# A decoder trunk on one core: softmax on negated scores, the sink as a column, one broadcast scaling, rotary's second product in one operation

## The chip, the core and the metric

The kernel runs on one core of a Trainium2 chip. The core's engines work side by side, each on a queue of its own in a fixed order: PE multiplies matrices, DVE does elementwise work and reductions, ACT evaluates functions and copies, POOL does elementwise work too, and SP issues the loads. They meet only where one waits for another's result. The metric is the device time of one execution in microseconds, the median of the runs.

## The reference, cut to what matters

Two layers over 256 tokens of width 1024, float32. Each is a half SwiGLU, a token mixer, a half SwiGLU, all on RMS-normed input with residuals. Layer 0 mixes with native sparse attention (16 heads of 64 in four groups; a compressed, a selected and a sliding-window branch with keys and values of their own, each weighted by a sigmoid gate). Layer 1 mixes with sliding-window attention of window 128, two key heads, and a sink logit per head:

```python
x1, x2 = jnp.split(x, 2, axis=-1)                       # rotary
out = jnp.concatenate([x1 * c - x2 * s, x2 * c + x1 * s], axis=-1)
...
s = jnp.where(mask, einsum(q, k) * scale, NEG)          # softmax with a sink
m = jnp.maximum(jnp.max(s, axis=-1, keepdims=True), sk)
e = jnp.exp(s - m)
p = e / (jnp.sum(e, axis=-1, keepdims=True) + jnp.exp(sk - m))
```

With 256 tokens, all of the selected blocks are taken, so the selected branch is causal attention over all keys, and so is the window of 512.

## The kernel before

The residual stays on chip, tokens on the partitions, in two tiles of 128 rows (`t` = 0, 1). Every large product runs on PE as three products of operands split into a high and a low part. A weight piece of 128x1024 is loaded by SP, its high part is cast (L150, mostly ACT), and its low part is a subtraction (L175), on DVE in one instruction or on POOL in two of 128x512. The names tell the product: `gu` and `dn` are the two of a SwiGLU, `nin`, `cmp`, `nout` the input, compression and output products of the first attention, `sin`, `sout` those of the second.

An attention layer is a list of steps in the code. `R` is a chunk of the input projection; `P` and `V` (or `A`) turn its result into rotated, transposed queries and keys by `rope` (L382) and `token_split`; `S` is `logits` (L425) for a group of four heads and a tile of rows; `M` is `weigh` and `heads_sum`, the products with the values. In the first layer `S` works on two branches (`nb` = 2, tiles `na_p`), in the second on one (`sa_p`). There are eight `S` steps in either layer, four groups by two tiles; a row is 128 keys long for `t` = 0 and 256 for `t` = 1.

Within `logits`: PE writes scores to PSUM (`na_s`, `sa_s`); for each head and branch one DVE instruction adds the mask, writes to SBUF and takes the row's greatest value (L443); a bias step makes the negated, scaled greatest value (L633 in the first layer; L741, L742, L744 with the sink in the second, and L745 for the sink's exponential on ACT); ACT takes one exponential a head, with its sum (L451); a scale step makes the reciprocal of the sums (and in the first layer multiplies by the gates, L636 and L638; in the second L749 adds the sink's exponential ahead of L750's reciprocal); then one scaling a head and branch (L461, or L459 on ACT) in place, mostly on DVE, some on POOL or ACT by a table. PE then transposes the probabilities (`na_t`, `sa_t`), ACT and DVE split them (`na_h`, `na_l`), PE multiplies with the values (`na_o`, `sa_o`).

A scheduler sets the order of every engine's queue when the kernel is built, from the order in the code, numbers on the steps that let them yield, and what depends on what. Between the `S` steps it places other work on the same queues: the weights' subtractions, the compression's GELU (`hid`, `ge_a`, `ge_b`, and `hidT`, the transpose on PE that follows it), the probabilities of the compressed branch (`cm`), rotary for the next group. At the start of each layer POOL raises the mean square to the power -1/2 (`n_y`, L231), and DVE makes the row scale and rotary's tables from it.

## Time and profile before

| | |
|---|---|
| median of 3 runs | 1046.49 us (1043.96 to 1047.28) |
| span of the profiled execution, first to last instruction | 1040.8 us; the profile gives no other time for it |
| PE busy | 997.2 us, 96% |
| DVE, ACT, POOL busy | 719.4, 554.7, 518.0 us |
| mean granted PE clock | 0.981 |
| first attention layer, about | 201 to 382 us |
| second attention layer, about | 751 to 848 us |

A row of the instruction views gives the start, the duration, the engine and line, the operation, the tiles written and read, and how many were merged; in brackets stands the engine's idle time before it and who ended it. Durations of neighbours on DVE overlap a little, so the distance between starts is what an instruction costs its queue. A row of the stretches gives the length, each engine's busy time in the order PE, weight loads, DVE, ACT, POOL, then the PE clock as a share of full speed and the DMA's share and rate.

### The profile page before, as it was taken

How to read it: one execution, taken by the hardware profiler on the slowest of the kernel's cores; microseconds unless marked ns; L12 is line 12 of the kernel's file. 1: busy time of each engine (PE TensorE's matmuls, PEld its weight loads, DVE VectorE, ACT ScalarE, POOL GpSimd, SP SyncE). 2: the span in 40 equal slices, each digit the busy share in tenths (PEclk: the TensorE clock that was granted, in tenths of full speed). 3: DMA queues.
4: the chain of work that ended last, by engine and by line, in shares of the span. 5: the costliest groups of instructions: out<-in, count | busy, mean ns of one | idle time of the engine just before them, and what ended most of it. 6: DMA issues, size and time to landing. Idle time of an engine off the chain costs nothing.

```text
span 1040.8 us, 16105 instructions
## 1 busy us (share of the span) xinstructions
PE 997.2 (96%) x5663; PEld 860.2 (83%) x5663; DVE 719.4 (69%) x1418; ACT 554.7 (53%) x1049; POOL 518.0 (50%) x504
## 2 busy tenths in 40 slices
PE   6999999998789999999999999999998899999996
PEld 5888888898778678888888888888897688888896
DVE  6777744478788987777445777754289888777533
ACT  5555544356458755565444555544457755555432
POOL 1675563457253417655631555572665326554543
PEclk9999999999889999999999999999999999999999
DMA  8665655533220336655555556546542156555551
GB/s 275 194 200 187 197 185 176 176 123 122 82 82 1 122 131 194 202 185 186 184 185 191 181 187 199 187 159 222 176 149 61 61 184 199 183 184 186 187 174 41
DMA packets 47328, 169.10 MB, mean 162 GB/s; under 512 B 5264, under 2 KB 5776, under 8 KB 47248
## 3 DMA queue, kind: packets, MB, share of 16 engines
q1 hardware_dynamic: 46512, 166.37, 49.8%
q10 hardware_dynamic: 576, 1.20, 0.4%
q8 instruction: 44, 0.72, 0.3%
q0 software_dynamic: 160, 0.52, 0.1%
q14 instruction: 36, 0.29, 0.1%
HBM read 167.02 MB, written 1.05 MB: 161 GB/s over the span
## 4 chain that ended last, share of the span: by engine, by line
PE 85%; DVE 8%; ACT 2%; POOL 2%; issue 2%; DMA 1%; POOLq 0%; DVEq 0%; ACTq 0%
PE gu L116 47%; PE dn L116 22%; PE nin L116 5%; DVE na_p L461 2%; PE nout L116 2%; PE na_o L116 2%; PE sout L116 1%; PE xt L191 1%; DVE sa_p L461 1%; PE sin L116 1%; PE na_s L116 1%; PE na_t L470 1%; ACT sa_p L451 1%; DMA x<-in_x_dram 1%; DVE sa_p L443 1%
## 5 line engine op out<-in xcount | busy, mean ns | idle before, releaser
L116 PE MATMUL gu<-xh,gu_h 128*128 128x512 f32 x1408 | 492.4, 396 | 2.8 <-DVE xh L200 2.8
L116 PE MATMUL gu<-xh,gu_l 128*128 128x256 f32 x1408 | 393.8, 280 | 0.0
L116 PEld LDWEIGHTS gu<-xh,gu_h 128*128 128x128 f32 x1408 | 264.8, 188 | 63.6 <-DVE xh L200 3.2
L116 PEld LDWEIGHTS gu<-xh,gu_l 128*128 128x128 f32 x1408 | 266.2, 189 | 0.5
L175 DVE TENSOR_TENSOR gu_l<-gu_r,gu_h 128x1024 fp32r<-128x1024 f32 (+1 forms) x177 | 237.4, 1342 | 27.0 <-ACT gu_h L150 26.7
L150 ACT CAST gu_h<-gu_r 128x1024 fp32r<-128x1024 f32 (+1 forms) x177 | 184.7, 1044 | 44.5 <-PE gu L116 21.8
L150 ACT CAST dn_h<-dn_r 128x1024 fp32r<-128x1024 f32 (+1 forms) x89 | 92.2, 1041 | 110.1 <-PE dn L116 102.6
L116 PE MATMUL dn<-dn_l,hh 128*128 128x512 f32 (+1 forms) x396 | 147.0, 371 | 0.0
L116 PE MATMUL dn<-dn_h,hh 128*128 128x512 f32 (+1 forms) x396 | 146.9, 371 | 0.0
L116 PE MATMUL dn<-dn_h,hl 128*128 128x512 f32 (+1 forms) x396 | 146.6, 370 | 0.0
L175 DVE TENSOR_TENSOR dn_l<-dn_r,dn_h 128x1024 fp32r<-128x1024 f32 (+1 forms) x56 | 72.1, 1291 | 99.6 <-ACT dn_h L150 99.6
L175 POOL TENSOR_TENSOR dn_l<-dn_r,dn_h 128x512 fp32r<-128x512 f32 x66 | 88.8, 1367 | 104.3 <-ACT dn_h L150 94.5
L155 POOL TENSOR_TENSOR ga<-g,rb 128x256 f32<-128x256 f32 x88 | 96.8, 1100 | 71.0 <-DVE g L356 48.5
L155 POOL TENSOR_TENSOR hl<-u,hh 128x256 fp32r<-128x256 f32 x66 | 80.3, 1217 | 49.9 <-ACT hh L150 25.3
L155 POOL TENSOR_TENSOR u<-u,rb 128x256 f32<-128x256 f32 x88 | 70.1, 796 | 66.6 <-DVE u L358 66.6
L360 ACT ACTIVATE th<-ga 128x256 f32<-128x256 f32 x88 | 36.8, 419 | 99.1 <-POOL ga L155 98.1
L116 PEld LDWEIGHTS dn<-dn_h,hl 128*128 128x128 f32 x396 | 74.8, 189 | 13.4
L116 PEld LDWEIGHTS dn<-dn_h,hh 128*128 128x128 f32 x396 | 74.7, 189 | 13.4
L116 PEld LDWEIGHTS dn<-dn_l,hh 128*128 128x128 f32 x396 | 74.8, 189 | 13.2
L150 ACT COPY g<-gu 128x256 f32<-128x256 f32 x88 | 32.7, 372 | 83.4 <-PE gu L116 82.8
L116 PE MATMUL nin<-nin_h,xh 128*128 128x256 f32 (+1 forms) x352 | 72.9, 302 | 1.4 <-DVE r_b L389 1.4
L362 DVE SCALAR_TENSOR_TENSOR ga<-th,ga 128x256 f32<-128x256 f32 x88 | 43.2, 491 | 36.2 <-ACT th L360 36.2
(243 smaller groups left out, 1483.5 us busy)
## 6 DMA issues: line engine op xcount, KB each, us to landing
gu_r<-in_wgu_dram SPq DMA_DIRECT2D x175, 512.0 KB, 4.1
dn_r<-in_wdn_dram SPq DMA_DIRECT2D x87, 512.0 KB, 3.5
nin_r<-in_nsa_in_dram SPq DMA_DIRECT2D x20, 512.0 KB, 3.5
sin_r<-in_swa_in_dram SPq DMA_DIRECT2D x10, 512.0 KB, 3.6
nout_r<-in_nsa_out_dram SPq DMA_DIRECT2D x8, 512.0 KB, 3.5
sout_r<-in_swa_out_dram SPq DMA_DIRECT2D x8, 512.0 KB, 3.6
cmp_r<-in_nsa_w_dram SPq DMA_DIRECT2D x4, 512.0 KB, 4.6
x<-in_x_dram SPq DMA_DIRECT2D x2, 256.0 KB, 5.1
```

The costliest lines, as they stand in the source:

```text
L116: nc.tensor.matmul(o, w, m, start=start, stop=stop)
L150: nc.scalar.copy(o, i)
L155: (nc.vector if pick(key) == "V" else nc.gpsimd).tensor_tensor(o, a, b, op)
L175: eng.tensor_tensor(lo[:, q:e], raw[:, q:e], hi[:, q:e], ALU.subtract)
L191: nc.tensor.transpose(ps[:, kk * S + t * P:kk * S + (t + 1) * P], x[t][kp // 2][:, c:c + P], ident)
L360: nc.scalar.activation(th, ga, AF.Tanh, scale=0.5)
L362: nc.vector.scalar_tensor_tensor(ga, th, 1.0, ga, ALU.add, ALU.mult)
L443: nc.vector.tensor_tensor_reduce(out=pr[b][:, hh, :], in0=ps[:, c:c + nk], in1=masks, scale=1.0, scalar=-3.0e38, op0=ALU.add, op1=ALU.max, ...
L451: nc.scalar.activation(pr[b][:, hh, :], pr[b][:, hh, :], AF.Exp, bias=nm[:, c:c + 1], scale=SCALE, accum_out=sm[:, c:c + 1])
L461: (nc.vector if which == "V" else nc.gpsimd).tensor_scalar(o, o, sc[:, c:c + 1], None, ALU.mult)
L470: nc.tensor.transpose(ps[:, hh * P:(hh + 1) * P], pr[:, hh, kt * P:(kt + 1) * P], ident)
```

## The change

Four edits, all in the attention layers.

Rotary's second product is one DVE instruction that reads the two halves in reversed order, where it was two.

The scores are written to SBUF negated and scaled, and the reduction takes the least value, for each head in a column of its own; that value is the exponential's bias as it stands, so the bias step is gone. In the second layer the reduction starts from the negated sink instead of a constant.

The sink is one more column of the tile of scores: rows are four elements longer, POOL copies the negated sinks there (`before`, L746 of the changed kernel), and the exponential runs over 129 or 257 elements, so that its sum includes the sink.

The scaling of a branch is one DVE multiply with the scales broadcast along the keys (L457 of the changed kernel), for four heads at once; POOL and ACT take no part in it any more.

```diff
             nc.vector.tensor_mul(a[:, :nh, :], v, tab[:, None, 0, :].to_broadcast([P, nh, HD]))
-            nc.vector.tensor_mul(b[:, :nh, :hf], v[:, :, hf:], tab[:, None, 1, :hf].to_broadcast([P, nh, hf]))
-            nc.vector.tensor_mul(b[:, :nh, hf:], v[:, :, :hf], tab[:, None, 1, hf:].to_broadcast([P, nh, hf]))
+            two = "p h (s e) -> p h s e"
+            nc.vector.tensor_mul(b[:, :nh, :].rearrange(two, s=2), v.rearrange(two, s=2)[:, :, ::-1, :],
+                                 tab[:, None, 1, :].to_broadcast([P, nh, HD]).rearrange(two, s=2))
...
-            pr = [pool.tile([P, 4, nk], F32, tag="p4", bufs=BUFS["p4"], name=f"{name}_p{b}") for b in range(nb)]
+            pr = [pool.tile([P, 4, nk + finish.extra], F32, tag="p4", bufs=BUFS["p4"], name=f"{name}_p{b}")
+                  for b in range(nb)]
+            finish.before(pr)
...
-                        nc.vector.tensor_tensor_reduce(out=pr[b][:, hh, :], in0=ps[:, c:c + nk], in1=masks, scale=1.0,
-                                                       scalar=-3.0e38, op0=ALU.add, op1=ALU.max,
-                                                       accum_out=mx[:, b * 4 + hh:b * 4 + hh + 1])
-            nm = sp.tile([P, nb * 4], F32, tag="nm", bufs=BUFS["nm"], name=f"{name}_nm")
-            extra = finish.bias(nm, mx)
+                        nc.vector.tensor_tensor_reduce(out=pr[b][:, hh, :nk], in0=ps[:, c:c + nk], in1=masks,
+                                                       scale=-SCALE, scalar=finish.least(hh), op0=ALU.add, op1=ALU.min,
+                                                       accum_out=mn[:, b * 4 + hh:b * 4 + hh + 1])
             for hh in range(4):
                 for b in range(nb):
                     c = b * 4 + hh
-                    nc.scalar.activation(pr[b][:, hh, :], pr[b][:, hh, :], AF.Exp, bias=nm[:, c:c + 1], scale=SCALE,
-                                         accum_out=sm[:, c:c + 1])
-            sc = finish.scale(sm, extra)
+                    o = pr[b][:, hh, :nk + (finish.extra > 0)]
+                    nc.scalar.activation(o, o, AF.Exp, bias=mn[:, c:c + 1], scale=-1.0, accum_out=sm[:, c:c + 1])
+            finish.scale(sm)
             for b in range(nb):
-                for hh in range(4):
-                    c = b * 4 + hh
-                    o, which = pr[b][:, hh, :], pick(f"sc{nb}")
-                    if which == "A":
-                        nc.scalar.activation(o, o, AF.Copy, scale=sc[:, c:c + 1])
-                    else:
-                        (nc.vector if which == "V" else nc.gpsimd).tensor_scalar(o, o, sc[:, c:c + 1], None, ALU.mult)
-            return pr
+                o = pr[b][:, :, :nk]
+                nc.vector.tensor_tensor(o, o, sm[:, b * 4:b * 4 + 4, None].to_broadcast([P, 4, nk]), ALU.mult)
+            return [p[:, :, :nk] for p in pr]
...
-                sink = prm[:, D_SINK:D_SINK + NH]
+                nsink = mp.tile([P, NH], F32, name="nsink")
+                nc.vector.tensor_scalar(nsink, prm[:, D_SINK:D_SINK + NH], -1.0, None, ALU.mult)
...
                 class Finish:
+                    extra = 4
                     def __init__(self, g):
-                        self.sink = sink[:, 4 * g:4 * g + 4]
-                    def bias(self, nm, mx):
-                        nc.vector.scalar_tensor_tensor(mx, mx, SCALE, self.sink, ALU.mult, ALU.max)
-                        nc.vector.tensor_scalar(nm, mx, -1.0, None, ALU.mult)
-                        es_ = sp.tile([P, 4], F32, tag="es", bufs=3, name="es")
-                        nc.vector.tensor_sub(es_, self.sink, mx)
-                        nc.scalar.activation(es_, es_, AF.Exp)
-                        return es_
-                    def scale(self, sm, es_):
-                        nc.vector.tensor_add(sm, sm, es_)
+                        self.sink = nsink[:, 4 * g:4 * g + 4]
+                    def before(self, pr):
+                        nk = pr[0].shape[2] - 4
+                        nc.gpsimd.tensor_copy(pr[0][:, :, nk:nk + 1], self.sink[:, :, None])
+                    def least(self, hh):
+                        return self.sink[:, hh:hh + 1]
+                    def scale(self, sm):
                         nc.vector.reciprocal(sm, sm)
```

In the first layer `extra` is 0, `before` does nothing, `least` is 3.0e38, and `scale` is the reciprocal and the product with the gates as before.

The order of the loads on SP is the same instruction for instruction. The other queues are scheduled anew in the two attention layers. Three places follow; a row gives the line, the operation, the tile written and those read, the shape, and how many follow each other.

DVE in the first layer, from the first of the GELU's multiplies to the one that the transpose `hidT` waits for (`na_p_2611` and `na_p_2612` are the scores of group 0, tile 1; `ge_b` is the GELU's result). Before:

```order
L638 TENSOR_TENSOR na_sm<-na_sm,gate 128x8
L572 TENSOR_TENSOR ge_a<-hid,ge_a 64x128
L461 TENSOR_SCALAR na_p_2611<-na_p_2611,na_sm 128x256 x4
L461 TENSOR_SCALAR na_p_2612<-na_p_2612,na_sm 128x256 x3
L572 TENSOR_TENSOR ge_a<-hid,ge_a 64x128
L175 TENSOR_TENSOR nin_l_2988<-nin_r_2986,nin_h_2987 128x1024
L574 TENSOR_SCALAR ge_a<-ge_a 128x128
L387 TENSOR_TENSOR k_a<-nin_0_2824,tab_2027 128x128
L576 TENSOR_TENSOR ge_b<-hid,ge_a 64x128 x2
```

And in the changed kernel (the same scores are `na_p_2597` and `na_p_2598`):

```order
L640 TENSOR_TENSOR na_sm<-na_sm,gate 128x8
L155 TENSOR_TENSOR r_sq<-r_a,r_sq 128x4x64
L457 TENSOR_TENSOR na_p_2597<-na_p_2597,na_sm 128x1024
L457 TENSOR_TENSOR na_p_2598<-na_p_2598,na_sm 128x1024
L566 TENSOR_SCALAR ge_a<-ge_a 128x128
L175 TENSOR_TENSOR nin_l_2812<-nin_r_2810,nin_h_2811 128x1024
L568 TENSOR_TENSOR ge_a<-hid,ge_a 64x128 x2
L175 TENSOR_TENSOR nin_l_2954<-nin_r_2952,nin_h_2953 128x1024
L570 TENSOR_SCALAR ge_a<-ge_a 128x128
L572 TENSOR_TENSOR ge_b<-hid,ge_a 64x128 x2
```

Seven scalings became two multiplies; one subtraction of `nin` (2812) now stands behind them where it stood ahead of them.

DVE in the second layer, at the first two `S` steps of the changed kernel (`sa_p_8188` is group 0, tile 0; `sa_p_8225` is group 0, tile 1; each L446 row is a head's reduction, the row behind it reads its result out):

```order
L446 ISA sa_p_8225,sa_mx<-sa_s_8227,cst,nsink 128x256
L446 ISA sa_mx 128x1
L752 RECIPROCAL sa_sm<-sa_sm 128x4
L446 ISA sa_p_8225,sa_mx<-sa_s_8234,cst,nsink 128x256
L446 ISA sa_mx 128x1
L457 TENSOR_TENSOR sa_p_8188<-sa_p_8188,sa_sm 128x4x128
```

The reciprocal of the first step, which waits for its four exponentials, stands behind two reductions of the second step and ahead of the other two. Before, the sink's addition and the reciprocal of that step came behind all four and behind rotary for the next queries.

POOL at the start of the second layer, in the changed kernel from the second to the third pair of `sin` subtractions and the norm's power:

```order
L175 TENSOR_TENSOR sin_l_7992<-sin_r_7990,sin_h_7991 128x512 x2
L746 COPY sa_p_8188<-nsink 128x4
L746 COPY sa_p_8225<-nsink 128x4
L746 COPY sa_p_8263<-nsink 128x4
L746 COPY sa_p_8324<-nsink 128x4
L746 COPY sa_p_8444<-nsink 128x4
L746 COPY sa_p_8537<-nsink 128x4
L746 COPY sa_p_8626<-nsink 128x4
L746 COPY sa_p_8734<-nsink 128x4
L175 TENSOR_TENSOR sin_l_7999<-sin_r_7997,sin_h_7998 128x512 x2
L231 TENSOR_TENSOR n_y<-n_v,mhalf 128x2
```

All eight copies stand together there, between work that before followed directly. The first waits for DVE's `nsink`, which DVE does behind the last residual of the SwiGLU.

More of the change, by code (lines that the diff above doesn't have):

```diff
@@ L630, in __init__ @@
                         self.g, self.t = g, t
[L632 to L635 removed]
+                    extra = 0
+                    def before(self, pr):
+                        pass
+                    def least(self, hh):
+                        return 3.0e38
+                    def scale(self, sm):
+                        gt = gate[:, self.t, 1:3, self.g * 4:self.g * 4 + 4]
+                        both = sm.rearrange("p (b h) -> p b h", b=2)
                         nc.vector.reciprocal(sm, sm)
[L637 to L640 removed]
+                        nc.vector.tensor_tensor(both, both, gt, ALU.mult)
                 oh, ol = out_tiles("nsa")
```

13 lines of the change are left out of this document (4 added, 9 removed).

## The prediction

> **What bounds the kernel now.** I read the page, then the stretches of the span, PE's waits with their times, and the DVE, POOL and ACT instructions ahead of each wait.
>
> ```profile
> span 1040.8 us, 16105 instructions
> PE 997.2 (96%) x5663; PEld 860.2 (83%) x5663; DVE 719.4 (69%) x1418; ACT 554.7 (53%) x1049; POOL 518.0 (50%) x504
> core 0: us, PE busy (x) PEld busy (x) DVE busy (x) ACT busy (x) POOL busy (x), PEclk, DMA share, GB/s
> 245.00:300.00 55.00, 44.26 (x298) 39.29 (x296) 48.97 (x155) 33.30 (x97) 28.01 (x27) 0.89 0.30 97
> 300.00:345.00 45.00, 42.61 (x267) 36.75 (x268) 37.54 (x128) 28.96 (x79) 16.52 (x21) 0.90 0.16 48
> 382.20:503.00 120.80, 120.80 (x699) 106.58 (x699) 93.32 (x148) 66.12 (x114) 70.69 (x71) 1.00 0.59 189
> 785.00:815.00 30.00, 24.61 (x148) 20.36 (x147) 27.48 (x106) 23.08 (x76) 12.68 (x13) 0.94 0.24 71
> ```
>
> The SwiGLU layers are PE's own (382 to 503: busy 120.80 of 120.80), and the change touches nothing there. What it touches lies in the attention layers, where PE idles 10.7 us of the 55 from 245 and 5.4 of the 30 from 785, and where DVE is the busiest of the others (48.97 of 55, 27.48 of 30). So the question is which PE gap ends on which DVE work:
>
> ```profile
> 265.40 0.47 PE L578 MATMUL hidT<-ident,ge_b 128*128 128x128 f32 x1 [5.33 <-DVE ge_b L576]
> 296.93 0.66 PE L403 MATMUL r_q<-ident,r_sq 128*128 128x128 f32 x4 [2.37 <-DVE r_sq L155]
> 327.28 0.50 PE L116 MATMUL na_o<-na_l,vv 128*128 128x512 f32 x1 [1.72 <-DVE na_l L474]
> 790.04 0.79 PE L116 MATMUL sa_o<-sa_l,vv 128*128 128x512 f32 x1 [3.36 <-DVE sa_l L474]
> 799.88 0.50 PE L116 MATMUL sa_o<-sa_l,vv 128*128 128x512 f32 x1 [1.05 <-DVE sa_l L474]
> 818.74 0.33 PE L470 MATMUL sa_t<-ident,sa_p 128*128 128x128 f32 x1 [0.75 <-DVE sa_p L461]
> 821.19 0.47 PE L470 MATMUL sa_t<-ident,sa_p 128*128 128x128 f32 x1 [0.90 <-DVE sa_p L461]
> ```
>
> Ahead of these stand, on DVE's queue, the scalings of L461 and the small bias operations, and beside them POOL:
>
> ```profile
> 249.63 1.27 DVE L633 TENSOR_SCALAR na_nm<-na_mx 128x8 f32<-128x8 f32 x1
> 250.81 1.21 DVE L175 TENSOR_TENSOR cmp_l<-cmp_r,cmp_h 128x1024 fp32r<-128x1024 f32 x1
> 256.89 5.29 DVE L461 TENSOR_SCALAR na_p<-na_p,na_sm 128x256 f32<-128x256 f32 x7
> 258.17 5.13 POOL L175 TENSOR_TENSOR nin_l<-nin_r,nin_h 128x512 fp32r<-128x512 f32 x4
> 262.52 1.87 DVE L175 TENSOR_TENSOR nin_l<-nin_r,nin_h 128x1024 fp32r<-128x1024 f32 x1
> 290.01 6.45 DVE L461 TENSOR_SCALAR na_p<-na_p,na_sm 128x256 f32<-128x256 f32 x7
> 323.31 3.32 DVE L461 TENSOR_SCALAR na_p<-na_p,na_sm 128x256 f32<-128x256 f32 x7
> 782.49 2.79 DVE L461 TENSOR_SCALAR sa_p<-sa_p,sa_sm 128x256 f32<-128x256 f32 x4
> 786.78 0.89 DVE L741 SCALAR_TENSOR_TENSOR sa_mx<-sa_mx,prm 128x4 f32<-128x4 f32 x1
> 787.80 1.09 DVE L742 TENSOR_SCALAR sa_nm<-sa_mx 128x4 f32<-128x4 f32 x1
> 797.96 1.20 DVE L742 TENSOR_SCALAR sa_nm<-sa_mx 128x4 f32<-128x4 f32 x1
> 812.64 0.62 DVE L461 TENSOR_SCALAR sa_p<-sa_p,sa_sm 128x256 f32<-128x256 f32 x2
> 817.34 3.79 DVE L461 TENSOR_SCALAR sa_p<-sa_p,sa_sm 128x128 f32<-128x128 f32 x3
> 817.32 4.97 POOL L175 TENSOR_TENSOR sout_l<-sout_r,sout_h 128x512 fp32r<-128x512 f32 x4 [7.55 <-ACT sout_h L150]
> ```
>
> Two scalings of 128x256 took 0.62 us at 812.64, 0.31 each. Seven took 5.29 us while four POOL subtractions of 1.28 us filled 5.13 us. Three of 128x128 took 3.79 us beside four more. Even a bias of 128x4 took 1.09 and 1.20 us. So a scaling and a POOL subtraction take turns, and each turn costs DVE up to about 1.25 us, however small its own operation is. That is what the change can alter: the number of DVE instructions that have to take a turn.
>
> **The change, part by part.** *Scaling.* 96 instructions (82 on DVE, 12 on POOL, 2 on ACT) become 24 on DVE, one for four heads: 12 of 128x1024, 12 of 128x512. The trace has no such broadcast multiply of this size; the nearest rows are subtractions of 128x1024. Free of POOL one took 1.21 us (1.14 to the start of the next), beside POOL 1.87. So a pair costs 2.3 to 3.7 us; I take 3.0 beside POOL, and 1.5 for a single one. Where POOL is quiet, four scalings of 0.31 are 1.24, the same as one multiply: nothing is lost there. The Trainium skill speaks against this part ("VectorE: DVE Perf Modes", The perf-mode tier table): fp32 tensor_scalar in SBUF runs at twice the rate, tensor_tensor only at one element a cycle. By it the quiet multiplies alone would cost DVE time, an estimated 0.4 us each from that page's cycle formulas; the 0.62 us for two scalings does not show such an advantage.
>
> *Bias.* All eight L633, and L741, L742, L744, L749 and ACT's es exponentials go. An exponential now needs only its own head's reduction. *Rope.* One DVE instruction of 28 pairs goes; each saves some 0.1 us beside waits that are taken below; nothing on its own. Should the reversed read cost double, it is about 0.2 us in each of 28, which the DVE's free time (6 us of 55 in its fullest stretch) covers.
>
> The path, gap by gap, beside the profiled span:
> 1. hidT, 5.33 us. Ahead of it on DVE: a bias of 1.1 us (to the next start) gone, the burst 5.29 to 3.0, rope 0.1. Saved 3.5.
> 2. r_q, 2.37 us: the burst 6.45 to 3.0 is more than the gap. Saved 2.4.
> 3. na_o, 1.72 us: 3.32 to 3.0. Saved 0.3.
> 4. sa_o, 3.36 us: 2.79 to 1.5, and 0.89 + 1.09 gone. Saved 3.0.
> 5. sa_o, 1.05 us: the bias of 1.20 gone. Saved 1.05.
> 6. sa_t, three gaps of 0.75 to 0.90, 2.4 together: 3.79 becomes one multiply of 128x512 behind one subtraction, 0.7 + 1.25. Saved 1.9.
>
> Together 12.1 us. Each long gap is also followed by a slow clock while PE is busy nearly throughout:
>
> ```profile
> 240.00:244.00 4.00, 3.93 (x21) 3.93 (x22) 2.17 (x20) 2.44 (x7) 0.73 (x1) 0.57 0.01 4
> 268.00:272.00 4.00, 4.00 (x21) 3.46 (x20) 2.02 (x4) 1.50 (x4) 2.06 (x2) 0.50 0.56 179
> 300.00:304.00 4.00, 4.00 (x18) 3.84 (x19) 3.21 (x8) 1.16 (x3) 2.73 (x3) 0.50 0.24 53
> 304.00:308.00 4.00, 4.00 (x21) 4.00 (x21) 2.77 (x11) 0.57 (x2) 1.96 (x2) 0.50 0.40 104
> 820.00:824.00 4.00, 3.10 (x9) 2.43 (x10) 3.83 (x11) 1.09 (x3) 2.29 (x2) 0.57 0.59 167
> ```
>
> Busy time times what the clock lacks: 4.0 x 0.50 behind gap 1, twice that behind gap 2, 3.1 x 0.43 behind gap 6: 7.3 us at most. But 240 to 244 has 0.57 as well, with no burst of L461 ahead of it, so a shorter gap need not spare the clock: I count half, 3.7. Gross 15.8 us.
>
> Two things work against it. First, PE then meets its next late operand. The DVE list has the gates, the splits and the weights' subtractions in the same queue, POOL's subtractions now wait for multiplies of 1.14 where they let scalings of 0.2 pass, and the new order puts a reciprocal, which waits for four exponentials, among the reductions of the following group. I let half of the gross reach the end, 7.9; with all of it or none of it as the bounds.
>
> Second, eight POOL copies of the sink stand ahead of sin_l and of the norm's n_y at the start of the second attention layer, behind DVE's nsink:
>
> ```profile
> L152 POOL CAST k_kd<-k_a 128x128 fp32r<-128x128 f32 x2 | 0.6, 290 | 0.0
> L916 POOL MEMSET const-float32-0.0<- 128x1 f32 x1 | 0.1, 98 | 0.2 <-issue 0.2
> 752.58 2.54 POOL L175 TENSOR_TENSOR sin_l<-sin_r,sin_h 128x512 fp32r<-128x512 f32 x2 [0.40 <-ACT sin_h L150]
> 755.68 0.69 POOL L231 TENSOR_TENSOR n_y<-n_v,mhalf 128x2 f32<-128x2 f32 x1 [0.56 <-DVE n_v L224]
> ```
>
> A copy of 128x4 lies between a memset of 128x1 (98 ns) and a cast of 128x128 (290 ns): eight cost 0.8 to 2.3 us. POOL has 0.40 + 0.56 us of slack there, so n_y, and the row scale, tables and queries behind it, come 0 to 1.4 us later. I take 0.5, in full, since PE already waits at the end of that chain.
>
> The sum: 1040.8 - 7.9 + 0.5 = 1033.4 for the span. The median of the runs, 1046.5, is 5.7 above the span; the page gives no other time for that execution. Forecast 1039.1.
>
> **The rivals.**
> - *All of it comes back* (chance 0.13): the next operands are ready and the clock keeps up. 12.1 + 7.3 - 0.5 = 18.9 us: 1027.6; with a third left behind, 1034. For it speaks that both attention layers lose DVE work throughout; against it, that PE's gaps have several releasers.
> - *The turns stay as long* (0.21). Each multiply waits for a whole subtraction: 2 x (1.14 + 1.28) = 4.8 for a pair, against 5.29 and 6.45. Then terms 1 and 2 shrink to 1.7 and 1.6, term 3 is lost and term 4 is 2.4: with 5 and 6 8.5 us, and no clock back. POOL's subtractions are held up as much, so I let a quarter arrive, 2.1, less 0.5 to 1.4 for the copies: 1044.9 to 1045.8, no measurable change. For it: POOL's 1.28 us at 258.17; against it: the subtraction of 1024 beside POOL that took 1.87, not 2.4. The Trainium skill states such a lock ("SBUF — State Buffer", Who interferes with whom): a DVE instruction with two SBUF inputs and a reading GpSimd instruction block each other for a whole instruction. The 1.87 agrees with a part of one turn.
> - *The reciprocal as a new wait, slower* (0.15):
>
> ```profile
> 775.40 0.29 DVE L443 CUSTOM_DVE_ANT_0 sa_p<-sa_s,cst 128x128 f32<-128x128 f32 x1
> 792.26 0.39 ACT L451 ACTIVATE sa_p<-sa_p,sa_nm 128x128 f32<-128x128 f32 x1
> 770.07 1.05 ACT L150 CAST sin_h<-sin_r 128x1024 fp32r<-128x1024 f32 x1 [0.62 <-PE sin L116]
> ```
>
>   Four exponentials take 4 x 0.39 + 0.19 us, four reductions 4 x 0.21. The reciprocal stands two reductions (0.34 each) later, so DVE waits about 0.4 us for it, and 1.4 if ACT has a weights' cast of 1.05 first, with the next group's reductions queued behind. Sixteen groups of 1.4 are 22 us; half of that on PE, 11, against a gain reduced to 5: 1052. It decides from about 1 us of wait a group. Against it: exponentials also start earlier now, since each waits for its own head alone.
>
> **How the numbers follow.** Forecast 0.51, around 1039, its own range 1033 to 1043. A run of this kernel can be told from no change at about 0.3%, 3.1 us, that is 1043.4 to 1049.6. Faster: the first rival and nearly all of the forecast, 0.63; same: the second rival and the edges, 0.23; slower 0.14. The range 1030 to 1049 leaves out most of the slower rival and the best end of the first.
>
> **What would show it.** Right: L457 on DVE at 1.2 to 1.9 us for 1024 with two where seven stood; the hidT gap below 2.5 us; no clock of 0.5 behind it; PE's idle time in what were 245 to 300 and 785 to 815 down from 16.1 us to below 10. Wrong: multiplies of 2.4 us beside POOL; DVE idle ahead of RECIPROCAL released by ACT's exponentials; n_y over 1 us later against the end of the last dn product; rope's second product above 0.5 us for 128x256.

## The result, and the profile after

The changed kernel takes 1029.4 us (median of four executions, 1028.6 to 1030.4) against 1046.5 us: ratio 0.9845, 95% interval 0.9829 to 0.9861. It is faster, as forecast, but by more than twice the forecast 7.4 us, and just outside the range that began at 1030. Further executions of the kernel before, 97 in all, had a median of 1042.4 us and ran from 1034 to 1049; 14 of the changed program had a median of 1029.5 and ran from 1027.6 to 1032.3. So the gain is about 13 us, with a ratio of 0.988 (0.984 to 0.992 and 0.985 to 0.992) in both later comparisons.

The page of the changed kernel:

```profile
span 1026.8 us, 15966 instructions
PE 986.3 (96%) x5663; PEld 854.1 (83%) x5663; DVE 705.8 (69%) x1293; ACT 555.6 (54%) x1039; POOL 516.7 (50%) x500
```

The span is 14.0 us shorter than before, PE's busy time alone 10.9 us, although PE's instructions are the same ones. That does not look like gaps closing. The stretches by layer, cut at the end of a `dn` product and at the first product of the next `gu`: first attention layer, second SwiGLU, third, second attention layer, fourth SwiGLU. First the kernel before, then the changed one; the columns are those of the prediction's stretches.

```profile
198.41:379.71 181.30, 164.30 (x1059) 143.87 (x1059) 149.97 (x440) 108.34 (x280) 84.28 (x82) 0.92 0.27 88
379.71:565.73 186.02, 186.01 (x988) 159.32 (x987) 122.25 (x184) 94.86 (x149) 92.45 (x89) 1.00 0.61 195
565.73:751.27 185.54, 185.54 (x989) 158.16 (x987) 118.18 (x177) 95.20 (x149) 100.40 (x97) 1.00 0.58 186
751.27:844.29 93.02, 83.45 (x530) 71.41 (x528) 78.79 (x241) 61.09 (x159) 44.85 (x46) 0.96 0.35 106
844.29:1032.15 187.86, 187.86 (x1111) 165.46 (x1109) 124.18 (x180) 92.49 (x148) 93.69 (x92) 1.00 0.52 168
```

```profile
198.18:374.24 176.06, 160.22 (x1060) 140.68 (x1059) 147.53 (x380) 109.32 (x280) 78.35 (x70) 0.95 0.32 97
374.24:559.06 184.82, 184.82 (x988) 158.19 (x987) 120.67 (x181) 94.65 (x149) 91.70 (x89) 1.00 0.63 191
559.06:743.75 184.69, 184.69 (x988) 157.94 (x987) 117.09 (x177) 95.25 (x149) 101.52 (x97) 1.00 0.62 186
743.75:833.51 89.76, 80.97 (x530) 70.40 (x528) 70.82 (x178) 60.01 (x149) 49.17 (x54) 0.98 0.38 114
833.51:1018.13 184.62, 184.62 (x1111) 164.46 (x1109) 123.73 (x180) 92.52 (x148) 98.23 (x92) 1.00 0.56 170
```

Three things are to be seen. PE's idle time (length less busy) in the attention layers falls only from 17.0 to 15.8 us and from 9.6 to 8.8. Its clock there rises from 0.92 to 0.95 and from 0.96 to 0.98. And the three SwiGLU layers, in which PE never waits and the change touches no instruction, are 1.20, 0.85 and 3.24 us shorter: 5.3 us together.

PE's longest gaps in the changed kernel's attention layers:

```profile
241.63 1.12 PE L415 MATMUL k_k<-ident,k_kd 128*128 128x128 f32 x4 [2.30 <-DVE qs L152]
264.51 0.39 PE L116 MATMUL nin<-nin_l,xh 128*128 128x256 f32 x1 [4.30 <-DVE nin_l L175]
289.97 0.58 PE L116 MATMUL nin<-nin_h,xh 128*128 128x256 f32 x1 [1.95 <-DVE r_b L389]
301.06 0.63 PE L404 MATMUL r_q<-ident,r_sq 128*128 128x128 f32 x4 [1.99 <-DVE qs L152]
757.78 0.33 PE L404 MATMUL q_q<-ident,q_sq 128*128 128x128 f32 x1 [2.19 <-POOL q_sq L155]
784.07 0.61 PE L116 MATMUL sa_o<-sa_h,vv 128*128 128x512 f32 x1 [3.52 <-ACT sa_h L150]
```

`hidT` no longer waits 5.33 us, but a `nin` product waits 4.30 at the same point, for the subtraction that now stands behind the multiplies. The first `sa_o` waits 3.52 where it waited 3.36, now for ACT. A gap of 2.19 us is new, ahead of the second layer's first queries. Of the prediction's list, the gaps of `na_o` (1.72 us) and of the second `sa_o` (1.05) and the three small ones of `sa_t` are gone in this trace.

### The profile page after: what moved, and what is told of

It is laid out like the page before. It is cut to its first block, busy times and chain, and to the rows that moved or that the text cites. A ratio compares the mean times of both kernels' runs of the same rounds, so it can differ in the third digit from the quotient of the medians.

```text
span 1026.8 us, 15966 instructions
## 1 busy us (share of the span) xinstructions
PE 986.3 (96%) x5663; PEld 854.1 (83%) x5663; DVE 705.8 (69%) x1293; ACT 555.6 (54%) x1039; POOL 516.7 (50%) x500
## 3 DMA queue, kind: packets, MB, share of 16 engines
HBM read 167.02 MB, written 1.05 MB: 164 GB/s over the span
## 4 chain that ended last, share of the span: by engine, by line
PE 84%; DVE 5%; POOL 4%; issue 3%; ACT 3%; DMA 1%; SPq 0%; POOLq 0%; DVEq 0%; ACTq 0%
PE gu L116 48%; PE dn L116 22%; PE nin L116 5%; PE nout L116 1%; PE sout L116 1%; PE na_o L116 1%; DVE na_p L457 1%; PE xt L191 1%; PE sin L116 1%; ACT sa_p L453 1%; PE na_t L466 1%; PE sa_o L116 1%; DMA gu_r<-in_wgu_dram 1%; POOL dn_l L175 1%; POOL sout_l L175 0%
## 5 line engine op out<-in xcount | busy, mean ns | idle before, releaser
L116 PEld LDWEIGHTS dn<-dn_h,hl 128*128 128x128 f32 x396 | 74.4, 188 | 12.9
L116 PEld LDWEIGHTS dn<-dn_l,hh 128*128 128x128 f32 x396 | 74.4, 188 | 12.3
```

The source lines that it names most:

```text
L116: nc.tensor.matmul(o, w, m, start=start, stop=stop)
```

## The experiments

Three theories were tried. *Turns*: DVE has fewer instructions that take turns with POOL, which is what the prediction rested on. *Bias*: without the bias step exponentials, reciprocals and scalings start earlier. *Order*: the scheduler laid the queues out anew, and the new order is the better one, whatever the operations cost. A fourth was forced by the stretches above: something in the unchanged SwiGLU layers.

The table has all 18 runs. Two measures are worked out from each trace: idle is PE's idle time in the layer, and clock is PE's busy time multiplied by what its granted clock lacks, summed over stretches of a quarter of a microsecond. Every ratio is to the kernel before on the same chip.

| kernel | us | ratio, 95% interval | first layer: length, idle, clock | second layer | SwiGLU 2 to 4 |
|---|---|---|---|---|---|
| before, trace of the prediction | | | 181.3, 17.0, 12.9 | 93.0, 9.6, 3.0 | 559.4 |
| before_again | 1044.0 | 1.002 (0.999 to 1.005) | 183.1, 17.0, 14.7 | 93.0, 9.6, 3.0 | 559.4 |
| before_moved | 1038.8 | 0.998 (0.995 to 1.001) | 176.8, 16.0, 8.4 | 92.0, 8.5, 3.1 | 556.5 |
| after, first trace | 1029.4 | 0.9845 (0.983 to 0.986) | 176.1, 15.8, 8.2 | 89.8, 8.8, 1.7 | 554.1 |
| after_again | 1029.2 | 0.988 (0.984 to 0.992) | 176.5, 16.8, 7.3 | 90.0, 9.1, 1.6 | 554.1 |
| new_order_again | 1029.7 | 0.988 (0.985 to 0.992) | 178.1, 15.2, 11.6 | 91.5, 9.2, 3.2 | 554.2 |
| after_pad | 1035.1 | 0.992 (0.989 to 0.995) | 178.3, 15.4, 11.3 | 90.9, 8.5, 3.4 | 556.9 |
| scale_only | 1040.0 | 0.998 (0.995 to 1.001) | 185.8, 20.2, 14.2 | 89.5, 9.0, 0 | 559.7 |
| bias_only | 1034.6 | 0.994 (0.992 to 0.997) | 181.8, 18.0, 11.3 | 88.2, 7.7, 1.7 | 555.9 |
| rope_only | 1045.9 | 1.006 (1.004 to 1.009) | 184.6, 19.5, 13.4 | 94.7, 9.7, 4.8 | 559.3 |
| after_heads | 1034.5 | 0.992 (0.990 to 0.995) | 179.0, 17.1, 9.0 | 92.9, 10.4, 3.1 | 554.2 |
| after_rope2 | 1036.7 | 0.997 (0.993 to 1.000) | 186.8, 18.6, 15.2 | 89.6, 9.1, 1.4 | 556.3 |
| late_copy | 1029.1 | 0.989 (0.984 to 0.995) | 178.3, 14.7, 12.3 | 88.3, 7.6, 1.7 | 554.2 |
| scale_old_order | 1036.8 | 0.995 (0.992 to 0.997) | 177.2, 16.6, 9.1 | 88.3, 8.0, 0 | 559.2 |
| bias_old_order | 1030.5 | 0.988 (0.985 to 0.992) | 182.9, 16.9, 14.8 | 86.0, 6.3, 0 | 556.5 |
| ops_old_order | 1032.8 | 0.991 (0.989 to 0.994) | 178.6, 15.5, 12.8 | 87.6, 6.9, 1.7 | 558.6 |
| heads_new_order | 1032.0 | 0.991 (0.988 to 0.993) | 176.5, 17.5, 6.7 | 92.2, 10.8, 1.5 | 554.1 |
| rope2_new_order | 1028.2 | 0.987 (0.984 to 0.990) | 175.0, 15.1, 8.1 | 88.3, 7.6, 1.7 | 554.2 |
| hybrid | 1028.4 | 0.986 (0.983 to 0.988) | 176.1, 14.6, 9.8 | 87.2, 6.6, 1.7 | 556.3 |
| best | 1029.4 | 0.988 (0.985 to 0.992) | 178.8, 14.9, 12.5 | 86.7, 5.7, 1.7 | 556.3 |

### Both kernels once more

> The kernel before, unchanged, as a control with a second trace. Theory 'attention alone' (the whole gain of 17 us is PE idle time and slow clock in the two attention layers): the time is 1046 again, the three SwiGLU stretches behind the first have their 185.9, 185.5 and 187.9 us of before within 0.3 us, and so the 185 of the changed kernel's have to be explained by the change. Rival 'PE's pace drifts' (matrix products follow each other every 229 to 241 ns, by stretches of the execution and not by the kernel): these stretches move by 1 us or more from one trace of the same kernel to the next, and the span with them.

> The changed kernel, unchanged, as a control. 'Attention alone': ratio 0.9845, SwiGLU stretches again 184.8, 184.9, 184.6 within 0.3 us. 'PE's pace drifts': the ratio is 0.983 to 0.990 and the SwiGLU stretches move by 1 us or more; the attention layers (dn's last product to the next gu's first) stay at 176.1 and 89.8 us within 1 us.

Neither theory had it. The SwiGLU layers have the same lengths in both traces of a kernel to within about 0.1 us, and differ by 5.3 us between the kernels: their pace goes with the program. (Only the first SwiGLU moves by itself, 187.9 and 190.9 us before.) What does move from one execution to the next is the clock in the first attention layer.

### Parts alone, with an order of their own

```diff
 # scale_only, on the kernel before; after_heads is the reverse on the changed kernel
-                for hh in range(4):
-                    ... tensor_scalar(o, o, sc[:, c:c + 1], None, ALU.mult)
+                nc.vector.tensor_tensor(o, o, sm[:, b * 4:b * 4 + 4, None].to_broadcast([P, 4, nk]), ALU.mult)
 # rope_only, on the kernel before; after_rope2 is the reverse on the changed kernel
-            nc.vector.tensor_mul(b[:, :nh, :hf], ...)
-            nc.vector.tensor_mul(b[:, :nh, hf:], ...)
+            nc.vector.tensor_mul(b[:, :nh, :].rearrange(two, s=2), v.rearrange(two, s=2)[:, :, ::-1, :], ...)
 # bias_only: both reverses at once on the changed kernel
```

> The kernel before with only the scaling changed to one broadcast multiply a branch; bias steps, the sink's exponential and rotary as before. 'Turns' (what counts is how many DVE instructions have to take turns with POOL): most of the gain, 1034 to 1038 us. 'Bias' (what counts is that exponentials start without the bias step): no more than 5 us of gain, 1041 or more.

> The changed kernel with the scaling put back to one instruction a head and branch, on DVE, POOL and ACT by the old table; the least value, the sink's column and rotary's single product stay. 'Turns': most of the gain is lost, 1039 to 1045 us. 'Bias': most of it stays, 1034 or less.

> The changed kernel with the scaling put back to one instruction a head and rotary's second product put back to two: what is left is the scores written negated, their least value as the exponentials' bias, and the sink's column. 'Bias' (taking the bias step off DVE lets the exponentials, the reciprocal and all that follows start earlier): the first attention layer, 181.3 and 183.1 us in the two traces of the kernel before, comes to 177 to 180 us and the hidT gap of 5.33 us is gone; the second stays near 93. Time 1034 to 1038. 'Turns': both attention layers stay within 1 us of before, time 1040 or more.

> The kernel before with rotary's second product as one operation, nothing else. By the prediction (nothing on its own): within 2 us of the kernel before, the attention layers within 1 us of 182 and 93. Rival 'any new order counts': a layer moves by 2 us or more although DVE only loses 28 short instructions, because the scheduler orders the queues anew.

> The changed kernel with rotary's second product put back to two operations. If rotary is worth nothing: 1029 to 1030 and attention layers of 176 and 90 us. 'Any new order counts': a layer moves by 2 us or more against the changed kernel.

The parts do not add. Against the kernel before, the scaling alone gives 2.3 us (its interval still holds 1), the bias and sink alone 5.7, rotary alone costs 5.6; put into the changed kernel, rotary gives 7.5 (measured on two chips) and the scaling 5.3. "Turns" and "bias" are not decided by this: scale_only came between the two, and bias_only has the time that "bias" expected but not the layers, 181.8 us in the first instead of 177 to 180 and 88.2 in the second instead of 93. A rotary edit that takes 28 short instructions off DVE is unlikely to cost 5.6 us as an operation, and its layers show gaps in new places: compared by the traces, at least 96 PE and 55 DVE instructions stand elsewhere in their queues. So with a scheduler in between, doing or undoing one part measures the part and a new order together.

### Parts alone, with the order kept

So the order was taken out of the scheduler's hands: a table holds every engine's queue of one kernel, and another kernel is built to it.

```diff
+def _keep_order(tc):
+    ...
+    for d in <the table>:
+        i = ins[k]
+        if i.engine in last:
+            tc.add_manual_dep(i, last[i.engine].name, info, reason="order")
+        last[i.engine] = i
...
         trunk_kernel(tc, *args)
+        _keep_order(tc)
```

> The changed kernel with its own order written out as a table and kept: the same program. 1029, ratio 0.984 to 0.992; anything else would mean that keeping the order costs something by itself.

Keeping the order costs nothing that can be measured. The same table then held the order of before or of the changed kernel, with the edits of the last section:

> All operations of the changed kernel, but every engine's queue in the order of the kernel before (the order is written out as a table and kept; a multiply stands where the first of its branch's scalings stood on DVE, a copy of the sink just ahead of its step's first reduction). 'Operations' (the gain comes from instructions that DVE no longer has to do, wherever they stand): first attention layer 176 to 178 us, second 89 to 90.5, time 1029 to 1033. 'Order' (the gain comes from the new places in the queues): 180 us or more and 92 or more, time 1037 or more.

> The kernel before with only the scaling changed to one multiply a branch, every queue in the order of before. By the prediction's terms 1, 2, 3, 4 and 6 the scaling is worth 2.3 (of 5.29 to 3.0) at hidT, 2.4 at r_q, 0.3 at na_o, 1.3 at sa_o and 1.9 at sa_t: gaps of about 3.0, 0, 1.4, 2.1 and 0.5 us, and 8 us off the span before anything is given back. If a multiply beside POOL takes 2.2 us, as a pair of 4.34 us showed in the run with the scaling alone: hidT stays above 4 us and the first layer within 1.5 us of 181.3 to 183.1; the second, where POOL is quieter, falls from 93.0 to 90 to 91.5.

> The kernel before with the negated scores, the least value as bias and the sink's column alone; scaling and rotary as before, every queue in the order of before. 'Operations': the bias step's part of the 8 to 10 us that all operations gave in the old order; by terms 1, 4 and 5 of the prediction 1.1 at hidT, 2.0 at the first sa_o and 1.05 at the second: first layer 1 to 2 us under 181.3 to 183.1, second 2 to 3 us under 93.0; time 1037 to 1040, less 2 to 4 more if 'place' holds. 'Order' (the bias step only gives where exponentials may be placed earlier): the layers within 1 us of before.

> The changed kernel with one scaling a head and branch again, by the old table of engines, every queue in the order of the changed kernel (four scalings where a multiply stood). 'Turns': DVE has four turns for one: first layer 3 us or more above the changed kernel's 176.1 to 176.5, second 1.5 us or more above 89.9, time 1034. 'Order': within 1.5 us in each, time 1029 to 1032, although the run with a new order of its own took 1034.5.

> The changed kernel with rotary's second product in two operations, every queue in the order of the changed kernel. With an order of its own it took 1036.7 us, 7 above the changed kernel. 'Order': nearly all of these 7 us were the order's: 1029 to 1031, the first layer within 1 us of 176.1 to 176.5. 'Operations': 28 short DVE instructions cost 7 us in any order: 1034 or more.

*All operations in the old order*: 1032.8 us, some 10 us of the gain against 1042.8 on that chip. The attention layers are as short together (266.3 us) as in the changed kernel (265.8 to 269.5). So the new order is not what made them short. In one trace each, the old order has 2.6 us more in the first layer, all of it lost to the clock (12.8 against 8.2), and 2.1 less in the second, where PE idles 1.9 us less. What the changed kernel has beyond it lies in the SwiGLU layers (558.6 us against 554.1).

*Rotary*: in the new order two operations instead of one change nothing that can be told (1028.2 us), and the same operations in an order of their own took 1036.7: the 7.5 us were the order's.

*Scaling*: worth 2.3 to 2.8 us in the new order. Neither theory held whole: the first layer stayed at 176.5 us, as "order" had it, and the second rose by 2.3, as "turns" had it. In the first, heads_new_order has seven scalings where the changed kernel's two multiplies take 4.54 us, and PE's idle time there is 17.5 us against 15.2 to 16.8, but less was lost to the clock (6.7 us against 7.3 to 11.6):

```profile
256.54 7.43 DVE L462 TENSOR_SCALAR na_p<-na_p,na_sm 128x256 f32<-128x256 f32 x7
```

So fewer turns are worth time on DVE, though half of what "turns" expected. In the old order, all other operations as before, the scaling shortens the second layer by 4.7 us, of which 3.0 are clock. In the first it saves 0.4 us of idle time (what else shortens that layer is the clock) and does nothing for `hidT`. DVE, POOL and PE of scale_old_order at that place:

```profile
257.58 4.39 DVE L456 TENSOR_TENSOR na_p<-na_p,na_sm 128x1024 f32<-128x1024 f32 x2
262.31 1.87 DVE L175 TENSOR_TENSOR nin_l<-nin_r,nin_h 128x1024 fp32r<-128x1024 f32 x1
256.14 6.96 POOL L175 TENSOR_TENSOR nin_l<-nin_r,nin_h 128x512 fp32r<-128x512 f32 x4 [0.93 <-ACT nin_h L150]
265.19 0.47 PE L573 MATMUL hidT<-ident,ge_b 128*128 128x128 f32 x1 [5.56 <-DVE ge_b L571]
```

Two multiplies beside POOL's subtractions took 4.39 us, against 5.29 for the seven scalings of before: 0.9 saved, not the 2.3 of the prediction, and the product with the gates ahead of them took 1.31 us where it had taken 0.17.

*Bias and sink*: in the old order this part alone brings 11.9 us. In the first layer it does nothing, and `hidT` waits exactly as before:

```profile
266.33 0.47 PE L578 MATMUL hidT<-ident,ge_b 128*128 128x128 f32 x1 [5.33 <-DVE ge_b L576]
785.77 0.50 PE L116 MATMUL sa_o<-sa_l,vv 128*128 128x512 f32 x1 [1.86 <-DVE sa_l L474]
```

In the second it shortens the layer by 7.0 us: 3.3 of idle time, and with the first `sa_o` gap down to 1.86 the clock never falls there (3.0). The SwiGLU layers give 2.9 more, for a reason that comes below. "Order" expected nothing of it and fell; "operations" missed the first layer. The ratio, 0.988, is that of the whole change: in the old order, scaling and rotary add nothing to it that shows (ops_old_order has 0.991).

### The sink's copies

```diff
-            finish.before(pr)
             for h0 in range(0, 4, per):
                 ...
+            finish.before(pr)
             for hh in range(4):
                 ... exponentials
```

> The changed kernel with the eight copies of the sink asked for just ahead of each step's exponentials instead of ahead of its scores, so that seven of the eight leave the start of the second layer; the order on PE and ACT stays nearly the same. If the copies hold up n_y, the tables and the queries: the gap of 2.19 us ahead of q_q falls to 0.7 or less and the second layer from 89.8 to 88.3 us or less, time 1028. If the transposes of the queries would wait for something else anyway: the gap stays above 1.5 us and the layer within 0.5 us.

The copies do hold up the second layer, though less by their own length than by a turn that POOL loses through them. POOL and DVE in the changed kernel:

```profile
744.89 1.04 POOL L746 COPY sa_p<-nsink 128x4 f32<-128x4 f32 x8 [0.18 <-DVE nsink L732]
748.53 0.69 POOL L231 TENSOR_TENSOR n_y<-n_v,mhalf 128x2 f32<-128x2 f32 x1
755.94 1.21 DVE L175 TENSOR_TENSOR sin_l<-sin_r,sin_h 128x1024 fp32r<-128x1024 f32 x1
756.02 1.71 POOL L155 TENSOR_TENSOR q_sq<-q_a,q_sq 128x256 fp32r<-128x256 f32 x1
```

POOL and PE in late_copy, and then in rope2_new_order, the kernel of the last section that keeps all eight copies at the start:

```profile
745.99 0.19 POOL L746 COPY sa_p<-nsink 128x4 f32<-128x4 f32 x1 [0.18 <-DVE nsink L732]
749.25 0.69 POOL L231 TENSOR_TENSOR n_y<-n_v,mhalf 128x2 f32<-128x2 f32 x1 [0.57 <-DVE n_v L224]
757.57 0.33 PE L404 MATMUL q_q<-ident,q_sq 128*128 128x128 f32 x1 [0.86 <-POOL q_sq L155]
```

```profile
753.65 0.72 POOL L155 TENSOR_TENSOR q_sq<-q_a,q_sq 128x256 fp32r<-128x256 f32 x1
754.42 0.33 PE L403 MATMUL q_q<-ident,q_sq 128*128 128x128 f32 x1 [1.14 <-POOL q_sq L155]
```

Eight copies take 1.04 us, 0.13 each. `n_y` starts 4.78 us into the layer with them and 4.40 without, and the subtraction `q_sq` that PE waits for starts 12.27 and 11.94 us into it: the copies themselves cost 0.3 to 0.4 us. The other 1.0 us is a turn. DVE's subtraction of `sin` starts 12.19 us into the layer in the changed kernel and 12.18 in late_copy. With the copies, `q_sq` comes 0.08 us behind it and takes 1.71 us; without them it comes first and takes 0.73. So PE's gap falls from 2.19 to 0.86 us, and the layer is 1.4 us shorter. In rope2_new_order `n_y` is as late as in the changed kernel (4.79), but DVE's subtraction starts at 12.60 us, behind `q_sq`: that takes 0.72 us, the gap is 1.14, and the layer has the 88.3 us of late_copy with all its copies in place.

The time of late_copy is no shorter: 1029.1 us. With 12.3 us the first layer lost more to the clock in this trace, so the 1.4 us are shown in the layer alone.

### The place in SBUF

The change drops the tiles `nm` and `es`, 192 bytes a partition. All that is allocated behind them lies 192 bytes lower, the hidden activations `hh` and `hl` of the SwiGLU among them, which the `dn` products read. Two kernels change the place of tiles and no operation of the layers, with the order kept:

```diff
 # after_pad, on the changed kernel
+        pad = sp.tile([P, 48], F32, tag="pad", bufs=1, name="pad")
+        nc.gpsimd.memset(pad, 0.0)
 # before_moved, on the kernel before
-            nm = sp.tile([P, nb * 4], ...)
+            nm = pool.tile([P, nb * 4], ...)
-                        es_ = sp.tile([P, 4], ...)
+                        es_ = mp.tile([P, 4], ...)
```

> The changed kernel, same operations in the same order, with an unused tile of 192 bytes a partition in the pool of the small tiles (one memset more on POOL at the start), so that the SwiGLU's hidden activations lie where the kernel before has them. 'Place' (the pace of the dn products hangs on where their operands lie): dn goes from 229 to 232 ns a product, the stretch from the second SwiGLU's end to the third's from 184.69 to 185.55 us, and the time rises by 2 to 4 us, to 1031 to 1033. 'No place' (the pace is set by something else): dn stays at 229, time 1029.

> The kernel before, same operations in the same order, with the bias step's tiles taken from the attention layers' own pools, so that the SwiGLU's hidden activations lie 192 bytes lower, where the changed kernel has them. 'Place': dn goes from 232 to 229 ns, the stretch from 185.55 to 184.69 us, and the time falls by 2 to 4 us, to 1038 to 1040, with not one instruction changed. 'No place': 1042, dn at 232.

The `dn` products of the third SwiGLU (x is the count, then the least, median and greatest duration in ns) in the kernel before, in before_moved, in the changed kernel, and in after_pad:

```profile
L116 PE MATMUL dn<-dn_l,hh x79: 390/393/477, 689.0 to 744.4; 128*128 128x512 f32 x79
```

```profile
L116 PE MATMUL dn<-dn_l,hh x80: 388/388/477, 688.1 to 743.3; 128*128 128x512 f32 x80
```

```profile
L116 PE MATMUL dn<-dn_l,hh x80: 388/388/477, 687.9 to 743.1; 128*128 128x512 f32 x80
```

```profile
L118 PE MATMUL dn<-dn_l,hh x81: 390/393/475, 687.9 to 744.7; 128*128 128x512 f32 x81
```

"Place" holds in both directions: 393 ns where the operands lie as before, 388 where they lie 192 bytes lower, with the same instructions in the same order. From start to start it is 232 and 229 ns, and it held in all 20 traces: 232 in the six with the old place, 229 in the fourteen with the new. The three SwiGLU layers follow by 2.9 us (559.4 to 556.5) and 2.8 (554.1 to 556.9). The times follow in direction, 3.7 us down and 5.4 us up (between two chips, and more than the 2 to 4 expected); for before_moved alone the interval still holds 1.

That leaves some 2.4 us of the 5.3. They are in `gu`, whose products of 512 and 256 columns by turns follow each other every 173 or 177 ns on the mean of six, one pace for the whole layer. In the fourth SwiGLU it is 177 in the kernel before and 173 in the changed one. It did not follow the 192 bytes, and it came as 177 in every kernel that has the second attention layer in the old order, as 173 in every one that has it in the new, and as 177 in four of the five that have orders of their own (late_copy, whose order on PE is nearly the new one, has 173). In ops_old_order the second SwiGLU has 177 as well. What chooses it stays open.

### Joining the better halves

> The changed kernel's operations with the queues of the first attention layer in the changed kernel's order (176.1 to 176.5 us) and those of the second in the order of the kernel before, with copies of the sink just ahead of each step's first reduction (87.6 us against 89.8 to 90.0). If the layers' orders are independent: 2 us under the changed kernel, 1027. If the pace of the last SwiGLU goes with the second layer's order (186.82 us with it, 184.62 without): all of it is lost, 1029.

> First layer: the changed kernel's operations but rotary's second product in two, in the changed kernel's order. Second layer: negated scores, least value and sink's column, but one scaling a head and rotary in two, in the order of the kernel before. If the layers' lengths in the single traces hold: first layer 175 to 176.5 us, second 86 to 87, so 3 us under the changed kernel, less about 2 for the slower pace of the last SwiGLU that came with the second layer's old order in every trace: 1027 to 1028. If those differences were the granted clock of single executions: 1029 or more.

The layers' orders are independent: hybrid has the first layer of the one kernel and the second of the other, with the least idle time after best. But the `gu` pace of 177 came with the second layer's old order, as feared. In best the first layer came to 178.8 us instead of 175 to 176.5, because 12.5 us were lost to the clock where the trace that it was built on had 8.1. Neither can be told from the changed kernel (1028.4 and 1029.4 against 1029.2 to 1029.7), so no version is shown to beat it.

## Why the prediction was right and wrong

In its direction it was right, and the two attention layers even gave what it forecast: 7.9 us with the clock, from 275.2 (two traces) to 267.3 us (three), against 7.4. But it was made up of other things, and a part was missing. The forecast of 1039.1 was 9.7 us too high: 5.3 of it are the SwiGLU layers, 3.8 the base, about 0.5 the attention layers. The same five traces, before to after, by what the time went to:

| | before | after | |
|---|---|---|---|
| PE idle in the attention layers | 26.6 | 25.0 | -1.6 |
| lost to the clock there | 16.8 | 11.2 | -5.6 |
| PE's work there at full clock | 231.9 | 231.1 | -0.8 |
| SwiGLU 2 to 4 | 559.4 | 554.1 | -5.3 |
| start, first SwiGLU, end | 208.4 | 206.3 | -2.1 |
| span | 1043.0 | 1027.7 | -15.3 |

**The step that failed: "the change touches nothing there".** The prediction set the SwiGLU layers aside because PE is busy in them throughout. Busy is not at a fixed pace: the dropped tiles moved the operands of `dn`, and `gu` changed its pace as well. The first is worth 2.9 us and shown by moving the tiles; the cause of the other 2.4 is open. With these 5.3 us the forecast span of 1033.4 becomes 1028.1, and the three traces have 1026.8 to 1029.4. No rival named it either.

**The base.** The 5.7 us between the span and the median were no cost that is paid each time. In the executions compared here the time is about 1.8 to 2.5 us above the span of the same execution, 1.8 for the first one of the changed kernel (1028.58 and 1026.8). So the profiled execution of before took about 1042.7 us, an ordinary one beside the median of 1042.4 over 97; the executions that gave 1046.5 lay above it. This step put 3.8 us too much on the forecast.

**Terms 1 to 6, 12.1 us gross.** With the operations alone, in the old order, the gaps went like this:

| | before | forecast saving | scaling alone | bias alone | all operations |
|---|---|---|---|---|---|
| 1 hidT | 5.33 | 3.5 | 5.56 | 5.33 | 3.50 |
| 2 r_q | 2.37 | 2.4 | 0.48 | 2.38 | 0.85 |
| 3 na_o | 1.72 | 0.3 | 0.96 | 1.72 | 0.96 |
| 4 sa_o | 3.36 | 3.0 | 0.36 | 1.86 | 0.96 |
| 5 sa_o | 1.05 | 1.05 | 1.25 | 0 | 0 |
| 6 sa_t, three | 2.43 | 1.9 | 0 | 1.61 | 0 |

All operations saved 10.0 us in these gaps, of 12.1. Terms 2 to 6 gave 8.2 us of 8.7: 2 and 4 were too large by 0.9 and 0.6, 3 and 6 too small by 0.5 each, 5 was right. Term 1 was mis-sized, 1.8 us for 3.5: beside POOL's subtractions the pair takes 4.4 to 4.5 us, not 3.0, nearly as the rival "the turns stay as long" had it with 4.8. The 1.1 us of bias bring nothing there alone, because another instruction took over the turn: in bias_old_order the subtraction `cmp_l` behind the place of L633 took 2.33 us instead of 1.21. DVE and POOL in the changed kernel, and the pair in ops_old_order:

```profile
255.00 1.23 DVE L640 TENSOR_TENSOR na_sm<-na_sm,gate 128x8 f32<-128x8 f32 x1
256.49 4.54 DVE L457 TENSOR_TENSOR na_p<-na_p,na_sm 128x1024 f32<-128x1024 f32 x2
262.16 2.30 DVE L175 TENSOR_TENSOR nin_l<-nin_r,nin_h 128x1024 fp32r<-128x1024 f32 x1
254.56 11.04 POOL L175 TENSOR_TENSOR nin_l<-nin_r,nin_h 128x512 fp32r<-128x512 f32 x6 [4.62 <-ACT nin_h L150]
```

```profile
259.60 2.34 DVE L457 TENSOR_TENSOR na_p<-na_p,na_sm 128x1024 f32<-128x1024 f32 x2
```

In ops_old_order POOL sat idle for 1.28 us, waiting for ACT's cast, when the pair began, and the pair went through in 2.34 us; there three small operations of DVE's queue around it took 1.24 to 1.28 us each.

Beside POOL a product of 128x8 takes 1.23 us and a multiply 2.27; free, a multiply takes 1.22. By the Trainium skill ("SBUF — State Buffer", Who interferes with whom) a DVE instruction with two SBUF inputs and a POOL instruction that reads SBUF block each other for a whole instruction. Here the trace agrees: 2.27 is the 1.22 of a free one and about 1.05 more. The 1.87 us on which the prediction leaned against that rule was the low end. Over the kernel the multiplies of 128x1024 average less, 1756 ns in the first layer and 1220 in the second:

```profile
L457 DVE TENSOR_TENSOR na_p<-na_p,na_sm 128x1024 f32<-128x1024 f32 x8 | 13.7, 1756 | 0.1
L457 DVE TENSOR_TENSOR sa_p<-sa_p,sa_sm 128x1024 f32<-128x1024 f32 x4 | 4.9, 1220 | 0.0
```

**Half of the gross reaches the end.** In the old order this was near: idle time fell by 4.2 us in all, because new gaps of 2.27 (`na_o`) and 2.61 us (`sa_s`, for ACT) opened and others grew, the next late operands that the prediction expected. In the changed kernel's own order only 1.6 are left. Its sign for this, idle time below 10 us in the two stretches that had 16.1, did not come; the changed kernel has 9.7 and 5.0 in the stretches with about the same work:

```profile
244.00:298.00 54.00, 44.34 (x311) 40.33 (x309) 47.05 (x123) 33.64 (x97) 28.11 (x21) 0.93 0.32 98
778.00:808.00 30.00, 25.02 (x153) 20.91 (x152) 23.40 (x74) 24.33 (x72) 12.06 (x13) 0.94 0.25 71
```

**The clock, 3.7 us counted and then halved.** It gave 5.6 in these traces. The granted clock falls to a half for 3.4 us at a time, one to four times in a row (four in rope_only alone), and each such step costs 1.7 us. Behind `hidT` there were three in both traces of before and in before_moved. Behind the `nin` gap that took its place there were one or two; the first trace has one:

```profile
265.50:269.00 3.50, 3.50 (x17) 3.24 (x16) 2.39 (x6) 0.14 (x1) 0.11 (x1) 0.51 0.87 289
269.00:272.50 3.50, 3.36 (x28) 2.77 (x28) 2.89 (x9) 2.76 (x8) 2.46 (x3) 1.00 0.39 158
```

So "no clock of 0.5 behind it" failed in the letter and came in the size. It is also luck. Behind the `r_q` gap of 2.37 us both traces of before have three steps (0.50 from 300 to 308 in the prediction's rows), and before_moved, same instructions, same order and the same gap of 2.37 us, has none:

```profile
294.71 0.66 PE L403 MATMUL r_q<-ident,r_sq 128*128 128x128 f32 x4 [2.37 <-DVE r_sq L155]
297.00:300.50 3.50, 2.57 (x20) 2.14 (x19) 3.50 (x9) 1.95 (x4) 2.98 (x3) 1.00 0.01 2
300.50:304.00 3.50, 3.50 (x30) 3.31 (x29) 3.50 (x15) 0.94 (x3) 2.08 (x3) 1.00 0.51 152
```

This is what spreads the times: four executions of scale_old_order with a mean clock of 0.988 took 1033.3 to 1034.5 us, its four with 0.981 took 1039.1 to 1040.8. Over all executions the mean clock is 0.982 before (97) and 0.986 after (14), about 4 us of the 13. Nor does every step stand behind a gap: in all 20 traces the clock also falls once to three times in a row from 218 to 224 us on, where PE had idled 0.03 us at most in the 6.8 us ahead. No gap of the prediction's list stands ahead of these, and what sets them is open. By the Trainium skill ("TensorE: Matmul & The Clock Gate", What's actually happening) the clock halves after an idle window of about 3.4 us and the window runs freely, so that one kernel varies from run to run. The steps and their luck agree; that a gap of 2.37 us can bring three of them does not fit an idle time of 3.4 us.

**The copies**, taken at 0.5, delay POOL by 0.3 to 0.4 us, as bounded. The prediction did not have the turn that `q_sq` loses to DVE by this, 1.0 us more; together they cost 1.4 us of the second layer. **The reciprocal as a new wait** came to 1.5 and 1.4 us in all:

```profile
L639 DVE RECIPROCAL na_sm<-na_sm 128x8 f32<-128x8 f32 x8 | 1.6, 195 | 1.5 <-ACT na_p L453 1.5
L752 DVE RECIPROCAL sa_sm<-sa_sm 128x4 f32<-128x4 f32 x8 | 1.4, 175 | 1.4 <-ACT sa_p L453 1.3
L389 DVE TENSOR_TENSOR r_b<-nin,tab 128x256 f32<-128x256 f32 x8 | 3.2, 412 | 0.0
```

That is 0.2 us a group, where 1 us was its threshold. **Rotary**, "nothing on its own", holds in a kept order, and the reversed read costs no more than the product beside it (412 ns and 412 for L387). "All of it comes back" named the number, 1027.6, but not what happened: it wanted the gaps gone.

## What to carry to other kernels

Before a gain is put down to what was edited, look at the stretches that the edit does not touch: a tile dropped or added moves others in SBUF, and here 192 bytes changed the pace of a product that PE never waited in. Where a scheduler orders the queues, undoing one part also draws a new order, worth 8 us here (1036.7 against 1028.2 us for the same operations); hold the order before parts are compared. And count a gap's price with the clock behind it, in steps, over several executions: a trace shows one of them, and the 25 of the kernel before on one chip ran from 1033.8 to 1047.8 us.

## What the runs showed of the hardware

DVE and POOL meet not only where one waits for the other's result: the product of 128x8 with the gates took 0.17 us in the kernel before, and 1.23 to 1.31 beside POOL's subtractions in three others. But taking turns is not a fixed price. In before_moved, which has the instructions and the order of the kernel before, the seven scalings ahead of `hidT` took 1.91 us instead of 5.29, and the gap was 2.40 instead of 5.33. First POOL in the kernel before, then DVE and POOL in before_moved:

```profile
256.93 1.27 POOL L461 TENSOR_SCALAR na_p<-na_p,na_sm 128x256 f32<-128x256 f32 x1 [1.27 <-DVE na_sm L638]
```

```profile
256.04 1.91 DVE L461 TENSOR_SCALAR na_p<-na_p,na_sm 128x256 f32<-128x256 f32 x7
256.08 2.67 POOL L461 TENSOR_SCALAR na_p<-na_p,na_sm 128x256 f32<-128x256 f32 x1 [1.28 <-DVE na_sm L638]
```

In before_moved POOL's one scaling waited until DVE's seven were through; in the kernel before it got its turn at once, and its subtractions then stood between DVE's scalings. Which of the two happens was not tried further; the tiles of the attention layers lie elsewhere in before_moved too. So term 1 rested on a burst that can cost 3.4 us less in another build of the same queues.

PE's pace in a stretch in which it waits for nothing has two values, kept for the whole product: 229 or 232 ns from product to product in `dn`, 173 or 177 in `gu`, at a granted clock of 1.00 throughout. In `dn` it hangs on where the operands lie in SBUF, shown by moving them by 192 bytes both ways; in `gu` its cause stays open. A reduction that starts from a column of SBUF instead of a constant takes longer, 476 ns against 408 for 128x256:

```profile
L446 DVE CUSTOM_DVE_ANT_0 na_p<-na_s,cst 128x256 f32<-128x256 f32 x32 | 12.1, 408 | 0.0
L446 DVE CUSTOM_DVE_ANT_0 sa_p<-sa_s,cst,nsink 128x256 f32<-128x256 f32 x16 | 7.2, 476 | 0.2
```
